# Sums of squares in two fp32r parts, and the first product of merge in the other PSUM bank

## The chip, the cores and the metric

The kernel runs on one core of a Trainium2 chip. What counts is the device time of one launch in microseconds (us). TensorE is called PE in the profile (its weight loads PEld), VectorE is DVE, ScalarE is ACT, GpSimd is POOL, and SyncE is SP, which issues nearly all DMAs.

## The reference

One encoder block in float32, for 1024 tokens and 16 meta tokens with 1024 features. The input is normed and projected; then two branches run side by side, are merged through gates, and a SwiGLU feed-forward block and a last norm follow. Cut to what the change touches:

```
y_a    = (softmax(q1 k1 + bias) - lam * softmax(q2 k2 + bias)) v     # branch A, 4 heads of 128
y_a    = y_a * rsqrt(mean(y_a^2 over the 128 of a head) + EPS) * gain * 0.8
y_b    = windowed attention with sinks, 8 heads of 64                # branch B
merged = sigmoid(ga) * (y_a @ w_ba) + sigmoid(gb) * (y_b @ w_bb)
h      = h + merged @ w_o
```

## The kernel before

**Arithmetic.** TensorE multiplies nearly everything in fp32r, a float32 of reduced precision. To keep the precision of float32, a factor is split into two parts: `split` (L118) has ScalarE copy the high part, rounded to fp32r, and another engine subtract it from the source, which leaves the low part. A product is then three matmuls: high by high, high by low and low by high. The matrix products of the gates, the output and the feed-forward block also go by Strassen-like schemes of seven products, which is where names such as product 1, 6, 5, 7, 3, 4 of a gate come from.

**Branch A** works on four heads `h` and, in each, eight tiles `t` of 128 tokens. For a tile and each of the two softmaxes m, `scores_a` makes 1040 scores in PSUM: two products of 352 columns into the tile `two` (one buffer) and one of 336 into a bank with the tag `sc` (three buffers in turn, which transposes and sums share). VectorE adds the bias and finds the least (L980 for the first 704, L984 for the rest), ScalarE takes the exponential with its sum (L988), VectorE computes the factor (L991, L993) and joins the two softmaxes (L994). `transpose_a` turns the result one tile later, in three banks of `sc` (L1006); ScalarE writes the high part (L1009) and VectorE the low part (L1010) into the tile `at`. `values_a` multiplies by the values, 25 matmuls for two tiles (L1019), and collects 512 tokens, half a head, in the PSUM bank `acc`. `normed_a` then norms that half: it is called eight times.

In `normed_a`, ScalarE squares the bank into `ysq` (L1026) and copies the bank, scaled, into `yg` (L1028). TensorE sums the squares over the partitions by multiplying each 128 columns of `ysq` by a column of ones, in fp32 (L1032). VectorE adds EPS (L1037), POOL takes the power -1/2 (L1038), TensorE spreads the factor over the partitions by four transposes (`apf`, L1043), VectorE multiplies (L1044), and SP stores the half to `ya_d`.

**Gate products** fill the gaps: `gate_steps` yields after three matmuls of 512 columns (L881), and the string `SLOTS` says where between the steps of branch A such a filling stands. POOL makes their weights (L799, L800). Products 5 and 3 of a gate accumulate in one PSUM bank, and 7 and 4 in another; ScalarE copies the bank out after product 5 as `q` (L902), VectorE after 7 (L905) and after 4 (L912).

**Order.** TensorE's order is that of the code (`manual_schedule`). The other engines' order, and that of SP's DMA queue, is made by a scheduler at build time, from its own estimates. Each engine then runs its instructions strictly in that order, and waits at one for what it needs.

**From branch A to merge.** When the last values are done, the pool of branch A is given back, and SP loads the first two weight tiles of branch B's product (L1139) and the eight half rows of y_b (L1142) into the tiles m0 and m1. ScalarE and POOL split the weights (`wbhb`), ScalarE and VectorE split y_b into four tiles `yb0` to `yb3`: `split_yb` does tiles 0 and 1, both halves, before the last gate products, and 2 and 3 behind the closing of the pool `gwork`, from which `ysq` and gate weights come too. Merge then goes through eight feature groups `o` and two token halves: `gated` (L1256) loads a gate, ScalarE takes the Sigmoid (L1260), and TensorE makes 12 matmuls (L721) into a bank that is taken in turn from two sets of four, `bank` and `bank_t`:

```
        n_gated[0] += 1
        ps = (ps_bank if n_gated[0] % 2 else ps_bank_t)(f"ppa_{o}_{half}_{i}")
        branch_mm(ps, w, src, tk)
```

These sets lie where branch A had its banks. After merge the output projection (L1537) begins with four banks of `bank`.

Of the kernel before, what the change touches and what calls it, by code (L numbers as in the profile page):

```python
# [19 lines left out]
P = 128  # L20
S = 1024
D = 1024
NM = 16
# [51 lines left out]
def encoder_block(ctx: ExitStack, tc: tile.TileContext, x, meta, norm_mix, w_in, lq1, lk1, lq2, lk2,  # L75
# [7 lines left out]
    def f32(ap):  # L83
        return ap.bitcast(F32)
# [24 lines left out]

    ident = const.tile([P, P], F32, name="ident")  # L110
    make_identity(nc, ident)
    ones = const.tile([P, 1], F32, name="ones")
    nc.gpsimd.memset(ones, 1.0)
    neg_half = const.tile([P, 4], F32, name="neg_half")
    const.tile([P, ROOM], F32, name="room")
    nc.gpsimd.memset(neg_half, -0.5)
# [881 lines left out]
    def transpose_a(h, t, s, at_):  # L998
        i = t % 2
        for b in range(3):  # L1000
            nb = 4 if b < 2 else 1
            kp = P
            pt = bank(psum2, "sc", f"apt_{h}_{t}_{b}", SC).rearrange("p (k t) -> p k t", k=4)
            for j in range(nb):
                k = 4 * b + j
                nc.tensor.transpose(pt[:kp, j, :], s[:, k * P:k * P + kp], ident)  # L1006
            hi = at_[:kp, 4 * b:4 * b + nb, 0, i * P:(i + 1) * P]
            lo = at_[:, 4 * b:4 * b + nb, 1, i * P:(i + 1) * P] if b < 2 else hi[:NM]
            nc.scalar.activation(hi, pt[:kp, :nb], AF.Copy)  # L1009
            nc.vector.tensor_tensor(lo, pt[:lo.shape[0], :nb], f32(hi)[:lo.shape[0]], ALU.subtract)  # L1010
            yield

    def values_a(h, t, v, at_, py):
        cols = slice(t % 4 // 2 * 256, t % 4 // 2 * 256 + 256)
        for part in range(3):
            for k in range(3 * part, 3 * part + 3):
                kp = P
                for j, (a, b) in enumerate(((0, 0), (0, 1), (1, 0)) if k < 8 else ((0, 0),)):
                    nc.tensor.matmul(py[:, cols], v[:kp, a, k, :], at_[:kp, k, b, :],  # L1019
                                     start=(k == 0 and j == 0), stop=(k == 8))  # L1020
            yield

    def normed_a(h, c, py):
        nm = f"{h}_{c}"
        ysq = gwork.tile([P, 512], F32, tag="ysq", name=f"ysq_{nm}", bufs=1)
        nc.scalar.activation(ysq, py, AF.Square)  # L1026
        yg = gstage.tile([P, 512], F32, tag="yg", name=f"yg_{nm}", bufs=2)
        nc.scalar.activation(yg, py, AF.Copy, scale=gsub)  # L1028
        yield
        pst = bank(psum2, "sc", f"apst_{nm}", SC)  # L1030
        for i in range(4):
            nc.tensor.matmul(pst[:, i:i + 1], ysq[:, i * P:(i + 1) * P], ones, start=True, stop=True)  # L1032
        f = small.tile([P, 4], F32, tag="af", name=f"af_{nm}", bufs=2)
        sums = sum_a.pop((h, c))
        e = small.tile([P, 4], F32, tag="ae", name=f"ae_{nm}", bufs=2)
        nc.vector.scalar_tensor_tensor(e, sums, EPS, sums, ALU.mult, ALU.mult)
        nc.vector.scalar_tensor_tensor(f, pst[:, 0:4], 1.0 / P, e, ALU.mult, ALU.add)  # L1037
        nc.gpsimd.tensor_tensor(f, f, neg_half, ALU.pow)  # L1038
        for _ in range(N_WAIT):
            yield  # L1040
        pf = bank(psum2, "sc", f"apf_{nm}", SC)
        for i in range(4):
            nc.tensor.transpose(pf[:, i * P:(i + 1) * P], f[:, i:i + 1].broadcast_to([P, P]), ident)  # L1043
# [40 lines left out]
    for n in range(AH * NT + T_LAG):  # L1084
        scoring, turning = iter(()), iter(())
        if n == 1:
            fill(2)
        if n < AH * NT:
            h, t = divmod(n, NT)
            if t == 0:  # L1090
                if not h:
                    ensure_g(2)
                ld = load_a(h)
                if not h:
                    ensure_g(4)
                load_v(h, ld[2])
                fill(G_HEAD if h else G_FIRST)
                if not h:
                    turn_into(2)
                    order_pool.__exit__(None, None, None)  # L1100
            if t % 2 == 0:
                at_ = apool.tile([P, 9, 2, 256], F32R, tag="at", name=f"at{h}_{t}", bufs=AT_BUFS)
# [34 lines left out]
    a11, asum, a12, w11 = m0[:, 0], m0[:, 1], m1[:, 0], m1[:, 1]  # L1137
    for o, raw in enumerate((a11[:, 2], asum[:, 0])):
        nc.sync.dma_start(raw.rearrange("p (c n) -> p c n", n=P), w_bb[:, o * P:(o + 1) * P].rearrange("(c p) n -> p c n", p=P))  # L1139
    for j in range(4):  # L1140
        for h in range(2):
            nc.sync.dma_start((a12, w11)[h][:, j], yb_d[j // 2][j % 2 * P:j % 2 * P + P, h * 512:h * 512 + 512])  # L1142
    ypool, close_ypool = pool("ypool")
    first_w = [branch_w(ypool, o, w_bb, "b", raw) for o, raw in enumerate((a11[:, 2], asum[:, 0]))]
# [4 lines left out]
    first_gt = [gate_tile(f"gt_0_{o}") for o in range(2)]  # L1149
    yb_t = []  # L1150

    def split_yb(p, j0):
        for j in (j0, j0 + 1):
            yb_t.append(p.tile([P, 2, S], F32R, name=f"yb{j}"))
        for h in range(2):
            cols = slice(h * 512, h * 512 + 512)
            for k in (j0, j0 + 1):
                split(yb_t[k][:, 0, cols], yb_t[k][:, 1, cols], (a12, w11)[h][:, k], nc.vector)

    ybpool, close_yb = pool("ybpool")  # L1160
    split_yb(ybpool, 0)
    while tail:
        step_tail()
        fill(1)
# [1 line left out]
        fill(1)  # L1166
    close_gwork()
    ybpool2, close_yb2 = pool("ybpool2")
    split_yb(ybpool2, 2)
    order_pe.__exit__(None, None, None)  # L1170
    fill(1000)
    close_psum2()
# [83 lines left out]
    def gated(i, o, half, w, src):  # L1256
        tk = slice(half * 512, half * 512 + 512)
        gt = first_gt.pop(0) if first_gt else gate_tile(f"gt_{i}_{o}_{half}")
        nc.sync.dma_start(gt, g_d[8 * i + o][:, tk])
        gate_ops.append(nc.scalar.activation(gt, gt, AF.Sigmoid))  # L1260
        n_gated[0] += 1
        ps = (ps_bank if n_gated[0] % 2 else ps_bank_t)(f"ppa_{o}_{half}_{i}")
        branch_mm(ps, w, src, tk)
        return gt, ps, tk

# [68 lines left out]
    sums_a.__exit__(None, None, None)  # L1334

    with tc.issue_after(gate_ops[-1].ins):
        nc.scalar.activation(small.tile([P, 1], F32, tag="rstd", name="silu_of_one"), ones, AF.Silu)
    close_ya()
    close_ypool()

# [530 lines left out]
```

## Time and profile before

| what | value |
|---|---|
| median of 3 runs | 1422.95 us (1422.85 to 1427.37) |
| the profiled execution | 1424.24 us |
| its span, first to last instruction | 1421.9 us |
| TensorE busy | 1401.0 us, 99% |
| VectorE, ScalarE, POOL busy | 914.8, 672.1, 636.7 us |
| granted TensorE clock | 0.998 |

The profile is that of one execution, so terms are summed against 1424.24 us. A row of the timeline has the start in us, the duration, the engine, the line, the operation, the written tile and the read ones, the shape and the count; in square brackets stands the idle time of that engine just before, and what ended it. A row with x4 stands for four such instructions one after the other.

### The profile page before, as it was taken

Reading aid. Unit: us, or ns where it says so; the run is one execution under the profiler, and the core shown is the slowest. Engines: PE = TensorE matmul, PEld = TensorE weight load, DVE = VectorE, ACT = ScalarE, POOL = GpSimd, SP = SyncE. Lnnn points to the kernel's source line nnn. Section 1 sums busy time; section 2 is a strip of 40 time slices with the busy share of each in tenths; the row PEclk is TensorE's granted clock in tenths of the full one; section 3 lists DMA queues with packets and bytes.
Section 4 is the critical chain, followed back from the end, with each engine's and each line's share of the span. In section 5 each row is a group of like instructions: output and inputs, shape, how many; then the busy total and the mean of one; then the engine's idle time right before and its main releaser. Section 6 shows DMA issues by size and latency. Waiting matters only on the chain.

```text
span 1421.9 us, 20667 instructions
## 1 busy us (share of the span) xinstructions
PE 1401.0 (99%) x7183; PEld 1202.7 (85%) x7183; DVE 914.8 (64%) x1584; ACT 672.1 (47%) x1284; POOL 636.7 (45%) x648
## 2 busy tenths in 40 slices
PE   9999999998999999999999999999999999999998
PEld 8998999987888888878888888888888888888886
DVE  6555666527787878666978956544555453787566
ACT  6355556435445555455346644333333333444454
POOL 4156865546677666322503055555545441000442
PEclk9999999999999999999999999999999999999999
DMA  8446565386896363296522724433333323954343
GB/s 235 92 128 184 154 199 160 106 290 225 259 318 211 105 209 105 68 342 198 149 103 90 207 90 148 148 106 98 101 111 104 97 97 110 353 186 144 120 128 144
DMA packets 194297, 228.27 MB, mean 161 GB/s; under 512 B 16824, under 2 KB 127360, under 8 KB 194192
## 3 DMA queue, kind: packets, MB, share of 16 engines
q1 hardware_dynamic: 192272, 224.11, 49.3%
q10 hardware_dynamic: 1920, 2.83, 0.7%
q8 instruction: 57, 0.93, 0.3%
q14 instruction: 48, 0.39, 0.1%
HBM read 152.48 MB, written 67.86 MB: 155 GB/s over the span
## 4 chain that ended last, share of the span: by engine, by line
PE 90%; DVE 4%; DMA 2%; ACT 1%; issue 1%; SPq 1%; POOL 1%; ACTq 0%; POOLq 0%; DVEq 0%
PE pg L1634 29%; PE pd L1738 14%; PE pg L881 8%; PE ppa L721 6%; PE po L1537 4%; PE pp_va L230 3%; PE pp_ka L230 3%; PE aps L977 3%; PE pp_qa L230 3%; PE apy L1019 3%; PE pp_qb L230 3%; PE bps L397 2%; PE po L1545 2%; PE bpy L437 1%; PE apt L1006 1%; PE bpt L432 1%
## 5 line engine op out<-in xcount | busy, mean ns | idle before, releaser
L1634 PE MATMUL pg<-t,wop 128*128 128x512 f32 x1056 | 242.5, 389 | 0.0
L1634 PEld LDWEIGHTS pg<-t,wop 128*128 128x128 f32 x1056 | 198.3, 188 | 41.1
L120 POOL TENSOR_TENSOR wop<-wf,wop 128x512 fp32r<-128x512 f32 x114 | 153.9, 1351 | 162.4 <-ACT wop L119 148.7
L1738 PE MATMUL pd<-ob,oa 128*128 128x512 f32 x924 | 210.1, 390 | 0.2 <-DVE ob L120 0.2
L1738 PEld LDWEIGHTS pd<-ob,oa 128*128 128x128 f32 x924 | 173.4, 188 | 36.8 <-DVE ob L120 1.0
L1634 PE MATMUL pg<-b,wop 128*128 128x512 f32 x792 | 183.3, 390 | 0.0
L1634 PEld LDWEIGHTS pg<-b,wop 128*128 128x128 f32 x792 | 148.5, 188 | 30.7
L881 PE MATMUL pg<-hT_hi,wopg 128*128 128x512 f32 x448 | 169.9, 400 | 2.7 <-POOL wopg L800 1.8
L119 ACT ACTIVATE wop<-wf 128x512 fp32r<-128x512 f32 x128 | 80.8, 633 | 73.4 <-PE pg L1634 44.3
L120 POOL TENSOR_TENSOR oa<-ra,oa 128x512 fp32r<-128x512 f32 x27 | 34.9, 1294 | 169.4 <-ACT oa L119 167.7
L119 ACT ACTIVATE oa<-ra 128x512 fp32r<-128x512 f32 x77 | 48.7, 632 | 109.0 <-PE pd L1738 50.8
L988 ACT ACTIVATE as<-as,amn 128x1040 f32<-128x1040 f32 x64 | 74.5, 1165 | 50.6 <-DVE amn L984 50.4
L881 PEld LDWEIGHTS pg<-hT_hi,wopg 128*128 128x128 f32 x448 | 84.3, 188 | 15.5 <-POOL wopg L800 2.2
L1411 DVE TENSOR_TENSOR s<-wf,wf 128x512 f32<-128x512 f32 x22 | 17.6, 798 | 112.2 <-DMA wf<-in_w_ff_up_dram 70.7
L977 PE MATMUL aps<-ak,aq 128*128 128x352 f32 (+1 forms) x384 | 86.6, 334 | 2.4 <-DVE amn L980 2.2
L881 PE MATMUL pg<-hT_lo,wopg 128*128 128x512 f32 x224 | 88.2, 394 | 0.0
L980 DVE CUSTOM_DVE_ANT_0 as<-aps,dist,far_a 128x704 f32<-128x704 f32 x64 | 60.3, 943 | 34.9 <-PE aps L977 34.6
L399 DVE CUSTOM_DVE_ANT_0 bs<-bps,tbx,nsink 128x432 f32<-128x432 f32 (+1 forms) x64 | 38.6, 629 | 61.6 <-PE bps L397 37.8
L1009 ACT ACTIVATE at<-apt 128x512 fp32r<-128x512 f32 (+1 forms) x96 | 45.4, 484 | 63.0 <-PE apt L1006 63.0
L977 PEld LDWEIGHTS aps<-ak,aq 128*128 128x128 f32 x384 | 64.2, 189 | 12.2 <-DVE amn L980 4.7
L409 POOL TENSOR_SCALAR bs<-bs,bdn 128x432 f32<-128x432 f32 (+1 forms) x64 | 36.9, 596 | 75.3 <-DVE bdn L407 34.4
L1019 PEld LDWEIGHTS apy<-at,av 128*128 128x128 f32 x400 | 54.2, 190 | 4.0
(321 smaller groups left out, 3131.1 us busy)
## 6 DMA issues: line engine op xcount, KB each, us to landing
ra<-aop SPq DMA_DIRECT2D x77, 256.0 KB, 2.7
wf<-in_w_ff_gate_dram SPq DMA_DIRECT2D x25, 512.0 KB, 3.8
wf<-in_w_ff_up_dram SPq DMA_DIRECT2D x25, 512.0 KB, 3.8
aop<-as SPq DMA_DIRECT2D x44, 256.0 KB, 2.1
w_c<-in_w_in_dram SPq DMA_DIRECT2D x17, 512.0 KB, 4.8
aop<-c SPq DMA_DIRECT2D x33, 256.0 KB, 2.0
ak<-ka_d SPq DMA_DIRECT2D x16, 520.0 KB, 6.5
t_d<-tst SPq DMA_DIRECT2D x16, 512.0 KB, 3.8
```

Of the source, the lines that this page charges most:

```text
L119: high = nc.scalar.activation(hi, src, AF.Copy)
L120: lo_eng.tensor_tensor(lo, src, f32(hi), ALU.subtract)
L230: product = nc.tensor.matmul(ps[:, :n], a[:, c, :], b[:, c, at:at + n], start=(u == 0), stop=(u == 3 * DC - 1))
L721: nc.tensor.matmul(ps, w[:, a, j, :], src(j, b, tk), start=(j == 0 and n == 0), stop=(j == 3 and n == 2))
L881: nc.tensor.matmul(ps, op[:, x, c, :], h[:, 4 * d + c, HALF[t]], start=(p in (1, 6, 7) and c == 0 and i == 0), stop=(p in (2, 6, 3, 4) and ...
L977: nc.tensor.matmul(ps[:, :n], qs[m][:, t * P:(t + 1) * P], ks[m][:, vv, k0:k0 + n], start=(vv == 0), stop=(vv == 1))
L980: nc.vector.tensor_tensor_reduce(s[m][:, 0:2 * n].rearrange("p (a k) -> p a k", a=2), two[:, :, :n], dist[:, u0:u0 + 2 * n].rearrange("p ( ...
L988: nc.scalar.activation(s[m][:, 0:L], s[m][:, 0:L], AF.Exp, bias=mn[:, m, 1:2], scale=-1.0, accum_out=dn[:, 1:2] if m else first_sum)
L1019: nc.tensor.matmul(py[:, cols], v[:kp, a, k, :], at_[:kp, k, b, :], start=(k == 0 and j == 0), stop=(k == 8))
L1537: nc.tensor.matmul(sets_o[p][u], oa[:, a, u * P:(u + 1) * P], ob[:, b, :], start=(p in (1, 5) and j == 0 and k == 0), stop=(p in (2, 3) an ...
L1634: nc.tensor.matmul(ps, op[:, x, c, :], b[:, y, c, :], start=(p in (1, 5) and c == 0 and n == 0), stop=(p in (4, 2, 3) and c == 3 and n == ...
L1738: nc.tensor.matmul(ps[u], oa[:, a, u * P:(u + 1) * P], ob[:, b, :], start=(p in (1, 2, 5) and j == 0 and k == 0), stop=(p in (2, 3, 4) and ...
```

## The change

- `ones` is a tile of two columns in fp32r.
- In `normed_a` the scaled copy `yg` comes first. Then ScalarE squares the PSUM bank in place, and `split` makes a high and a low part of the squares in `ysq` (twice as large, fp32r): ScalarE copies, VectorE subtracts. TensorE multiplies each 128 columns of both parts by the two columns of ones and accumulates; VectorE reads every second column of the result.
- The tile `at` has 17 slots of 256 columns in place of 18; the slot that is left out was not used.
- The y_b rows are loaded by halves (the first half of all four tiles, then the second), and `split_yb` is called by halves too: tiles 0 and 1, first half, before the last gate products, and behind them tiles 2 and 3 first half, 0 and 1 second half, 2 and 3 second half.
- The banks of merge begin with `bank_t`.

```diff
-    ones = const.tile([P, 1], F32, name="ones")
-    nc.gpsimd.memset(ones, 1.0)
+    ones = const.tile([P, 2], F32R, name="ones")
+    nc.gpsimd.memset(f32(ones), 1.0)
...
-            hi = at_[:kp, 4 * b:4 * b + nb, 0, i * P:(i + 1) * P]
-            lo = at_[:, 4 * b:4 * b + nb, 1, i * P:(i + 1) * P] if b < 2 else hi[:NM]
+            tk = slice(i * P, i * P + P)
+            if b < 2:
+                hi, lo = (at_[:, 8 * b + u:8 * b + 7 + u:2, tk] for u in range(2))
+            else:
+                hi, lo = at_[:, 16:17, tk], at_[:NM, 16:17, tk]
...
-        ysq = gwork.tile([P, 512], F32, tag="ysq", name=f"ysq_{nm}", bufs=1)
-        nc.scalar.activation(ysq, py, AF.Square)
         yg = gstage.tile([P, 512], F32, tag="yg", name=f"yg_{nm}", bufs=2)
         nc.scalar.activation(yg, py, AF.Copy, scale=gsub)
+        nc.scalar.activation(py, py, AF.Square)
+        ysq = gwork.tile([P, 2, 512], F32R, tag="ysq", name=f"ysq_{nm}", bufs=1)
+        split(ysq[:, 0], ysq[:, 1], py, nc.vector)
         yield
         pst = bank(psum2, "sc", f"apst_{nm}", SC)
         for i in range(4):
-            nc.tensor.matmul(pst[:, i:i + 1], ysq[:, i * P:(i + 1) * P], ones, start=True, stop=True)
+            for u in range(2):
+                nc.tensor.matmul(pst[:, 2 * i:2 * i + 2], ysq[:, u, i * P:(i + 1) * P], ones, start=(u == 0), stop=(u == 1))
...
-        nc.vector.scalar_tensor_tensor(f, pst[:, 0:4], 1.0 / P, e, ALU.mult, ALU.add)
+        nc.vector.scalar_tensor_tensor(f, pst[:, 0:8:2], 1.0 / P, e, ALU.mult, ALU.add)
...
-    for j in range(4):
-        for h in range(2):
+    for h in range(2):
+        for j in range(4):
             nc.sync.dma_start((a12, w11)[h][:, j], yb_d[j // 2][j % 2 * P:j % 2 * P + P, h * 512:h * 512 + 512])
...
-    def split_yb(p, j0):
+    def open_yb(p, j0):
         for j in (j0, j0 + 1):
             yb_t.append(p.tile([P, 2, S], F32R, name=f"yb{j}"))
-        for h in range(2):
-            cols = slice(h * 512, h * 512 + 512)
-            for k in (j0, j0 + 1):
-                split(yb_t[k][:, 0, cols], yb_t[k][:, 1, cols], (a12, w11)[h][:, k], nc.vector)
+
+    def split_yb(j0, h):
+        cols = slice(h * 512, h * 512 + 512)
+        for k in (j0, j0 + 1):
+            split(yb_t[k][:, 0, cols], yb_t[k][:, 1, cols], (a12, w11)[h][:, k], nc.vector)
...
-    split_yb(ybpool, 0)
+    open_yb(ybpool, 0)
+    split_yb(0, 0)
...
-    split_yb(ybpool2, 2)
+    open_yb(ybpool2, 2)
+    for j0, h in ((2, 0), (0, 1), (2, 1)):
+        split_yb(j0, h)
...
-        ps = (ps_bank if n_gated[0] % 2 else ps_bank_t)(f"ppa_{o}_{half}_{i}")
+        ps = (ps_bank_t if n_gated[0] % 2 else ps_bank)(f"ppa_{o}_{half}_{i}")
```

More of the change, by code (lines that the diff above doesn't have):

```diff
@@ L1018, in values_a @@
                 for j, (a, b) in enumerate(((0, 0), (0, 1), (1, 0)) if k < 8 else ((0, 0),)):
-                    nc.tensor.matmul(py[:, cols], v[:kp, a, k, :], at_[:kp, k, b, :],
+                    nc.tensor.matmul(py[:, cols], v[:kp, a, k, :], at_[:kp, 2 * k + b, :],
                                      start=(k == 0 and j == 0), stop=(k == 8))
@@ L1101, in encoder_block @@
             if t % 2 == 0:
-                at_ = apool.tile([P, 9, 2, 256], F32R, tag="at", name=f"at{h}_{t}", bufs=AT_BUFS)
+                at_ = apool.tile([P, 17, 256], F32R, tag="at", name=f"at{h}_{t}", bufs=AT_BUFS)
             s = [None, None]
@@ L1336, in encoder_block @@
     with tc.issue_after(gate_ops[-1].ins):
-        nc.scalar.activation(small.tile([P, 1], F32, tag="rstd", name="silu_of_one"), ones, AF.Silu)
+        nc.scalar.activation(small.tile([P, 1], F32, tag="rstd", name="silu_of_one"), f32(ones)[:, 0:1], AF.Silu)
     close_ya()
```

## Prediction

> **What bounds the kernel now.** I read the page first: span, busy time by engine.
>
> ```profile
> span 1421.9 us, 20667 instructions
> PE 1401.0 (99%) x7183; PEld 1202.7 (85%) x7183; DVE 914.8 (64%) x1584; ACT 672.1 (47%) x1284; POOL 636.7 (45%) x648
> ```
>
> TensorE (PE) is the bound nearly everywhere, so an edit counts only by the TensorE work that it removes and by the waits of TensorE that it makes or ends. The second view is the list of TensorE's waits (what waited, for whom, us in total, times, longest).
>
> ```profile
> PE apt L1006 <- DVE at L1010: 2.3, 4, 0.8
> PE aps L977 <- DVE amn L980: 2.2, 7, 0.4
> PE ppa L721 <- DVE g L912: 0.8, 1, 0.8
> ...
> PE pd L1738 <- DVE ob L120: 0.2, 1, 0.2
> ```
>
> The first two lie in branch A, 310 to 597 us: there VectorE (DVE) is at times late, so VectorE has no room in those places. The third is the first product of merge, which the change is aimed at. The third view is the busy time by stretch (stretch, length, PE busy with count, then PEld, DVE, ACT, POOL).
>
> ```profile
> 616.00:700.00 84.00, 84.00 (x372) 69.39 (x371) 62.27 (x82) 38.51 (x68) 29.23 (x19) 1.00 0.69 224
> ```
>
> After 616 us TensorE does not stop (84.00 of 84.00), and of the list's waits only the last, 0.2 us at L1738, lies later. So every microsecond that TensorE loses before 616 us is one at the end: nothing gives it back.
>
> **Part 1: the sums of squares.** There are eight column groups (four heads, two halves), `normed_a` once each. Before: four fp32 products with one column. After: eight fp32r products with two columns. From the timeline, TensorE alone, in one of the middle groups:
>
> ```profile
> 437.32 0.95 PE L1032 MATMUL apst<-ones,ysq 128*128 128x1 f32 x8
> 438.13 0.63 PE L1006 MATMUL apt<-ident,as 128*128 128x128 f32 x4
> ```
>
> The four fp32 products stand there as eight matmuls, and with their weight loads they hold TensorE for 438.13 - 437.32 = 0.81 us, 0.10 each. The trace of before has no fp32r product with so few columns. The nearest rows are these eight themselves (0.10) and the transposes, which also load 128x128 weights per short matmul (four in 0.60 with the drain of the last, as at 441.73 below: at most 0.15 each). So eight after cost about 0.8 too: I take 0. The bounds are a gain of half, 0.4 us a group (3.2 in all), and a loss of 0.1 a group.
>
> [...]
>
> What is added: on ScalarE (ACT) the Copy of the high half, and Square now goes second, behind the scaled copy; on VectorE one subtract of 128x512 from PSUM. All 14 rows that follow are one middle group (head 1, first half) in the timeline:
>
> ```profile
> 432.30 0.60 ACT L1026 ACTIVATE ysq<-apy 128x512 f32<-128x512 f32 x1 [0.93 <-PE apy L1019]
> 432.79 0.69 ACT L1028 ACTIVATE yg<-apy,gsub 128x512 f32<-128x512 f32 x1
> 434.15 0.57 DVE L984 CUSTOM_DVE_ANT_0 as<-aps,far_m,amn 128x336 f32<-128x336 f32 x1
> 434.75 0.69 DVE L905 TENSOR_TENSOR g<-pg,q 128x512 f32<-128x512 f32 x1
> 435.83 0.95 DVE L980 CUSTOM_DVE_ANT_0 as<-aps,dist,far_a 128x704 f32<-128x704 f32 x1 [0.40 <-PE aps L977]
> 436.71 0.69 DVE L1010 TENSOR_TENSOR at<-apt,at 128x512 fp32r<-128x512 f32 x1
> 437.31 0.56 DVE L984 CUSTOM_DVE_ANT_0 as<-aps,far_m,amn 128x336 f32<-128x336 f32 x1
> 437.92 1.16 ACT L988 ACTIVATE as<-as,amn 128x1040 f32<-128x1040 f32 x1 [0.99 <-DVE amn L984]
> 439.20 0.27 DVE L993 TENSOR_SCALAR adn<-asum,adn,neglam 128x1 f32<-128x1 f32 x1 [0.73 <-ACT as L988]
> 439.32 0.88 PE L977 MATMUL aps<-ak,aq 128*128 128x352 f32 x4
> 439.51 1.30 DVE L994 SCALAR_TENSOR_TENSOR as<-as,adn,as 128x1040 f32<-128x1040 f32 x1
> 440.73 0.87 DVE L1010 TENSOR_TENSOR at<-apt,at 128x512 fp32r<-128x512 f32 x2
> 441.73 0.60 PE L1006 MATMUL apt<-ident,as 128*128 128x128 f32 x4
> 442.52 0.91 PE L977 MATMUL aps<-ak,aq 128*128 128x352 f32 x4 [0.19 <-DVE amn L980]
> ```
>
> The squares themselves are in time: scaled copy at 432.30, Square at 432.9, high half by 434.2, low half by 434.9, and `apst` reads them at 437.32, 2.4 us of cover. The price is what stands behind the subtract on VectorE. In the changed program's order it sits just ahead of L984 at 434.15, which moves by 0.7 to 434.85. The 0.40 of idle time before L980 at 435.83 takes up part, and about 0.35 arrives at the exponential (437.92) and at L993 (439.20, now 439.55).
>
> Then comes what the diff doesn't tell. The order of VectorE is made by a scheduler, and with the extra work it turns: in five of the seven middle groups L980 of the next tile now stands ahead of L994 or of the L1010 behind it (before, it stood after both). L980 needs the four score products at 439.32 + 0.88 = 440.20, so it runs 440.2 to 441.2. L994 starts at 441.2 instead of 439.51, L1010 ends at 443.1, and the transposes that wait for its PSUM slot go from 441.73 to 443.1. The score products behind them then needn't wait and start about 0.45 later, at 443.55 instead of 442.52: **+1.0 us**. In the two groups whose order is kept only the 0.35 to 0.5 passes through, I take 0.4. Middle groups: 5 x 1.0 + 2 x 0.4 = +5.8. Bounds: nothing (VectorE's idle time swallows it all), and 7 x 1.5 = 10.5 where a turned L994 also runs long, as this one did beside a POOL instruction:
>
> ```profile
> 366.85 2.25 DVE L994 SCALAR_TENSOR_TENSOR as<-as,adn,as 128x1040 f32<-128x1040 f32 x1
> ```
>
> One small gain: in the last tile L994 no longer stands behind a 16x128 L1010 of 0.27 while TensorE waits, -0.2.
>
> **Part 2: the eighth group and merge's start.** Here nothing but gate products is left to cover waits. The rows run from the last sums to the first product of merge; the last two are the eight loads of yb by source line, with their time from issue to landing.
>
> ```profile
> 600.47 3.88 SPq L1142 DMA_DIRECT2D m<-yb_d  x8
> 601.33 1.01 POOL L1038 TENSOR_TENSOR af<-af,neg_half 128x4 f32<-128x4 f32 x1 [1.22 <-DVE af L1037]
> 602.49 0.63 ACT L119 ACTIVATE wbhb<-m 128x512 fp32r<-128x512 f32 x1 [2.10 <-DMA m<-in_w_branch_b_dram]
> 603.07 0.60 PE L1043 MATMUL apf<-ident,af 128*128 128x128 f32 x4
> 603.20 1.28 POOL L120 TENSOR_TENSOR wbhb<-m,wbhb 128x512 fp32r<-128x512 f32 x1 [0.86 <-ACT wbhb L119]
> 604.68 0.63 ACT L119 ACTIVATE yb<-m 128x512 fp32r<-128x512 f32 x1 [0.74 <-DMA m<-yb_d]
> 607.93 0.56 ACT L902 COPY q<-pg 128x512 f32<-128x512 f32 x1
> 608.89 0.40 PE L881 MATMUL pg<-hT_lo,wopg 128*128 128x512 f32 x1
> 611.40 1.68 ACT L119 ACTIVATE yb<-m 128x512 fp32r<-128x512 f32 x3 [2.31 <-DMA m<-yb_d]
> 613.09 1.28 ACT L1260 ACT_TABLE_LOAD   x1
> 614.38 0.63 ACT L1260 ACTIVATE gt<-gt 128x512 f32<-128x512 f32 x1
> 615.11 25.25 PE L721 MATMUL ppa<-yb,wbhb 128*128 128x512 f32 x110 [0.78 <-DVE g L912]
> L1142 SPq DMA_DIRECT2D m<-yb_d x8: 430/430/499, 600.5 to 603.9; - x8
> DMA to landing us min/median/max: 4.1/5.4/8.1
> ```
>
> Three things move. First, the squares: ready some 1.8 us later, and no cover. Second, on POOL the power (601.33) now stands behind both subtracts for merge's weights, which wait for a load: the first starts at 603.20, so the power ends at 603.2 + 2 x 1.29 + 1.01 = 606.8, and the transposes at 603.07 start at 606.9: +3.8, the first delay inside it. Third, on ScalarE the copy of the gate bank q (607.93) now stands behind the table load, the first Sigmoid and the four copies for yb tiles 2 and 3. TensorE's product (7, 3) accumulates into that bank and waits for the copy. The Sigmoid's input is queued behind the eight yb loads, of which the last lands at 603.9 + 8.1 = 612.0; with one more transfer, 612.6. Sigmoid 0.55, four copies at 1.68 / 3 = 0.56 each, q 0.56: done at about 615.9. The second matmul of (7, 3) goes from 608.89 to 616.1: +7.2, which contains the +3.8.
>
> Merge's first product in the other bank no longer waits for VectorE's L912: -0.78. Its inputs are long split by then. Sum of part 2: +7.2 - 0.8 = **+6.4**. If the Sigmoid's input came much earlier, the power's +3.8 would stay: +3.0 is the lower bound; above, a DMA later by a microsecond gives +7.4.
>
> **At nothing.** The weights tile of 17 slots holds the same slices, so the 400 value products read as before. The last product of merge now lies in the bank of the fourth product of the output projection:
>
> ```profile
> 702.40 12.86 PE L1537 MATMUL po<-ob_o,oa_o 128*128 128x512 f32 x56
> 702.67 0.69 DVE L1299 TENSOR_TENSOR gt<-gt,ppa 128x512 f32<-128x512 f32 x1 [1.52 <-PE ppa L721]
> ```
>
> Nine matmuls (9 x 0.23 = 2.1 us) lie ahead of that fourth product, and VectorE reads the bank by 703.4, 1.0 after 702.40; without the cover it would cost 1.0.
>
> **Sum.** 5.8 - 0.2 + 6.4 = +12.0. The profiled execution took 1424.24 us (2.3 around its span), and would take 1436.2; the median of the three runs lies 1.3 below it, so 1422.95 + 12.0 = 1435.0.
>
> **The rivals.**
> - *Half of it* (one of the two parts is covered): +5.6 or +6.4, so 1428.6 to 1429.4. For it: VectorE is idle for 0.40 and 0.73 in the rows above; against it: TensorE waited for VectorE in these groups before already.
> - *No slower, or a little faster*: the sums' matmuls cost half. That is 8 x 0.4 = 3.2, with merge's wait 4.0: 1419.0. It decides only if the subtract finds idle time in each middle group, and if in the eighth the weight subtracts on POOL start by 599.5 (603.07 - 1.01 - 2 x 1.29) instead of 603.2, with q no later than now. [...] Without the half, the bank alone is 1422.2, which is also the case that the change does nothing else that shows.
> - *Worse*: the turned L994 meets POOL as at 366.85, 0.95 more in each of five groups, +4.8: 1439.8 or above.
>
> **How the numbers follow.** Forecast 0.55, with a range of its own of 1431 to 1439; half 0.20; no slower 0.15; worse 0.10. About 0.3%, 4.3 us, is what a measurement of this kernel can tell from no change: bounds 1418.7 and 1427.2. Faster 0.04 (only the end of the third case), same 0.16 (the rest of it, and the half case where it falls short), slower 0.80. Leaving out the no-slower case and the top of the worst one, the range is 1425 to 1441.
>
> **What would show it.** Right: the wait of `apt` for L1010 in the profile after is several us longer, with L980 run ahead of L994; `apst` still about 0.8 us a group; the power on POOL ends after two weight subtracts; the copy q on ScalarE ends just before the (7, 3) product, with a TensorE wait of some us on it; no wait at merge's first product. Wrong: `apst` at 0.4 us, no longer waits in branch A, or q finished before TensorE asks for it.

## The result, and the profile after

| | us |
|---|---|
| changed kernel, median of 6 runs | 1433.41 (1431.25 to 1434.54) |
| kernel before, median of 6 runs | 1423.29 (1422.52 to 1427.37) |
| ratio | 1.0064, 95% interval 1.0049 to 1.0078 |
| profiled execution after (before) | 1431.29 (1424.24) |

The change costs 0.64%. The forecast of 1435.0 is 1.6 above the median. The profiled execution is one of the two shortest of the six: it shows 7.0 of the 10.1 us by which the medians differ, and the rest has to be found elsewhere (below: the clock).

The page's head, span and TensorE's busy time: TensorE has 1.6 us more of busy time, and waits for the rest.

```profile
span 1429.5 us, 20694 instructions
...
PE 1402.6 (98%) x7183; PEld 1203.8 (84%) x7183; DVE 915.8 (64%) x1592; ACT 675.8 (47%) x1292; POOL 637.7 (45%) x648
```

TensorE's waits after (us in total, times, longest). L1010 is L1013 now.

```profile
PE apt L1006 <- DVE at L1013: 8.0, 8, 1.9
PE apf L1048 <- POOL af L1043: 2.0, 1, 2.0
...
PE ppa L721 <- DVE g L912: 0.8, 1, 0.8
...
PE aps L977 <- DVE amn L980: 0.7, 2, 0.4
PE apt L1006 <- DVE as L994: 0.5, 1, 0.5
```

The wait of `apt` for the subtract of its low part went from 2.3 to 8.0 us, that of `aps` from 2.2 to 0.7, that of `apt` for L994 from 1.7 to 0.5. The wait for the power (`apf`) is new, and so are those for the squares (`apst`) and for q, which stand in the rows further down. Merge's wait for L912 was to go, and is there unchanged.

The timeline after, in the middle group that the prediction worked through (start in us, duration, and in brackets the idle time before):

```profile
437.38 0.95 PE L1037 MATMUL apst<-ones,ysq 128*128 128x2 f32 x8
438.19 0.66 PE L1006 MATMUL apt<-ident,as 128*128 128x128 f32 x4
...
440.34 0.95 DVE L980 CUSTOM_DVE_ANT_0 as<-aps,dist,far_a 128x704 f32<-128x704 f32 x1 [0.70 <-PE aps L977]
...
441.21 1.30 DVE L994 SCALAR_TENSOR_TENSOR as<-as,adn,as 128x1040 f32<-128x1040 f32 x1
442.43 0.87 DVE L1013 TENSOR_TENSOR at<-apt,at 128x512 fp32r<-128x512 f32 x2
...
443.26 0.63 PE L1006 MATMUL apt<-ident,as 128*128 128x128 f32 x4 [1.27 <-DVE at L1013]
443.64 0.89 PE L977 MATMUL aps<-ak,aq 128*128 128x352 f32 x4
```

L980 runs ahead of L994 as foreseen, the transposes start at 443.26 (worked out: 443.1) and the score products behind them at 443.64 (443.55). The sums take 438.19 - 437.38 = 0.81 us, as before.

The timeline after, from the eighth group's sums to merge:

```profile
602.45 0.27 PE L1037 MATMUL apst<-ones,ysq 128*128 128x2 f32 x1 [0.81 <-ACT ysq L119]
603.18 0.94 PE L1037 MATMUL apst<-ones,ysq 128*128 128x2 f32 x7 [0.45 <-DVE ysq L120]
...
605.10 2.52 POOL L120 TENSOR_TENSOR wbhb<-m,wbhb 128x512 fp32r<-128x512 f32 x2 [3.62 <-ACT wbhb L119]
607.58 1.45 POOL L1043 TENSOR_TENSOR af<-af,neg_half 128x4 f32<-128x4 f32 x1
609.09 1.12 PE L1048 MATMUL apf<-ident,af 128*128 128x128 f32 x4 [2.00 <-POOL af L1043]
616.05 0.56 ACT L902 COPY q<-pg 128x512 f32<-128x512 f32 x1
616.66 0.50 PE L881 MATMUL pg<-hT_hi,wopg 128*128 128x512 f32 x1 [0.72 <-ACT q L902]
623.18 1.19 PE L721 MATMUL ppa<-yb,wbhb 128*128 128x512 f32 x4 [0.78 <-DVE g L912]
```

Squares late, power behind two weight subtracts, q just ahead of product (7, 3): all in the order that was forecast. What was not forecast is in the view of stretches (stretch, length, busy times of PE, PEld, DVE, ACT, POOL, then the granted clock, DMA share, GB/s):

```profile
604.00:605.00 1.00, 1.00 (x7) 0.84 (x7) 0.16 (x1) 0.61 (x1) 0.00 (x0) 1.00 0.84 288
605.00:606.00 1.00, 1.00 (x4) 0.80 (x3) 0.00 (x0) 0.56 (x2) 0.90 (x1) 0.61 1.04 240
...
611.00:612.00 1.00, 1.00 (x4) 0.81 (x3) 0.74 (x2) 0.80 (x2) 0.00 (x0) 0.50 1.04 402
612.00:613.00 1.00, 1.00 (x5) 0.79 (x5) 1.00 (x2) 0.98 (x2) 0.00 (x0) 0.98 1.07 404
```

From about 605.2 to 612.0 TensorE's clock is 0.5. That begins some 1.2 us after the sums that waited for the squares; in the kernel before, the clock was 1.0 in the same work.

The start of one and the same matmul in both profiles, subtracted, shows where the time goes. At the first group (346 us) the changed kernel is 0.5 ahead, at the last sums (599) 1.4 behind, at merge 8.1, at the end 7.5. So the seven middle groups cost 1.9 us in this execution, and the eighth with merge's start 6.7, of which 6.1 had come by the last row ahead of the wait for q. For all twelve experiments these differences are in the table below. A clock cut is a stretch at a granted clock of 0.5, as above: 3.4 us in the profiles of sums, halves, last_old, power, qfirst, both, mended, filled and high_pin_bank, 6.8 in those of the changed kernel and of pin.

| kernel | median us | ratio to before | middle groups, us (clock cuts in them) | eighth group and merge's start, us |
|---|---|---|---|---|
| changed | 1433.41 | 1.0064 | +1.9 (0) | +6.7 |
| sums | 1435.38 | 1.0083 | +3.9 (1) | +5.8 |
| halves | 1425.71 | 1.0005 | -0.6 (0) | +1.3 |
| last_old | 1430.50 | 1.0037 | +6.9 (2) | -0.3 |
| high | 1427.86 | 1.0023 | +1.7 (0) | -0.3 |
| power | 1433.77 | 1.0060 | +4.2 (1) | +4.9 |
| qfirst | 1431.51 | 1.0052 | +1.9 (0) | +2.8 |
| both | 1431.86 | 1.0052 | +4.3 (1) | +1.8 |
| bank | 1423.56 | 0.9993 | -0.4 (0) | -0.2 |
| pin | 1429.35 | 1.0042 | +1.8 (0) | +5.2 |
| mended | 1428.34 | 1.0030 | +1.2 (0) | +1.8 |
| filled | 1429.89 | 1.0039 | +3.2 (1) | +1.8 |
| high_pin_bank | 1422.54 | 0.9988 | -0.6 (0) | -1.9 |

Each ratio is to runs of the kernel before on the same chip (medians 1423.29 to 1424.45), and its interval reaches 0.0008 to 0.0017 to either side. The two columns of differences come from one execution each, which need not be a typical one: those of high and qfirst are the shortest of their kernels (1424.45 and 1429.47), that of power is the longest (1434.17). Kernels that change nothing in the middle (halves, bank) show -0.4 to -0.6 there, so that much of a difference means nothing.

### The profile page after: what moved, and what is told of

It reads as the page before. It is cut to its first block, busy times and chain, and to the rows that moved or that the text cites. A ratio compares the mean times of both kernels' runs of the same rounds, so it can differ in the third digit from the quotient of the medians.

```text
span 1429.5 us, 20694 instructions
## 1 busy us (share of the span) xinstructions
PE 1402.6 (98%) x7183; PEld 1203.8 (84%) x7183; DVE 915.8 (64%) x1592; ACT 675.8 (47%) x1292; POOL 637.7 (45%) x648
## 4 chain that ended last, share of the span: by engine, by line
PE 88%; DMA 4%; DVE 4%; issue 1%; ACT 1%; SPq 1%; POOL 0%; ACTq 0%; DVEq 0%; POOLq 0%
PE pg L1643 29%; PE pd L1747 15%; PE pg L881 7%; PE ppa L721 6%; PE po L1546 4%; PE pp_ka L230 3%; PE pp_va L230 3%; PE pp_qa L230 3%; PE aps L977 3%; PE apy L1022 3%; PE apt L1006 2%; PE bps L397 2%; PE pp_qb L230 2%; PE po L1554 2%; PE bpy L437 1%; PE bpt L432 1%
## 5 line engine op out<-in xcount | busy, mean ns | idle before, releaser
L980 DVE CUSTOM_DVE_ANT_0 as<-aps,dist,far_a 128x704 f32<-128x704 f32 x64 | 60.5, 945 | 38.7 <-PE aps L977 38.4
```

The source lines that it names most:

```text
L980: nc.vector.tensor_tensor_reduce(s[m][:, 0:2 * n].rearrange("p (a k) -> p a k", a=2), two[:, :, :n], dist[:, u0:u0 + 2 * n].rearrange("p ( ...
```

## The experiments

**sums: the first part alone.** The kernel before with the new `normed_a`, `ones` and `at`; loads, splits and banks untouched.

> The kernel before with the first part of the change alone: squares in two parts, two columns of ones, the tile at of 17 slots (its room goes to the larger ysq). The loads and splits of yb and the banks are as before. Theory: the whole loss is here, 1431 to 1434 against 1423; POOL's power stands behind both weight subtracts and the copy q behind the table load and four yb copies, though nothing of yb was touched, and the second matmul of product (7, 3) is 7 to 8 us later than before. Rival, the halves of yb make the late q: only the middle groups' loss is left, +1.3 to +3.5, 1424.5 to 1427.

Measured: 1435.38, ratio 1.0083 (1.0066 to 1.0100). The timeline of this kernel:

```profile
611.04 1.47 POOL L1043 TENSOR_TENSOR af<-af,neg_half 128x4 f32<-128x4 f32 x1
...
619.62 0.49 PE L881 MATMUL pg<-hT_hi,wopg 128*128 128x512 f32 x1 [1.64 <-ACT q L902]
```

The power and q are late with nothing of yb touched. So the whole loss lies in the first part of the change, and the scheduler's new orders in the eighth group come from it. The numbers are above the expected ones: the time by 1.4 us, and the product that waits for q comes 11.0 us later than before, of which 5.3 were lost ahead of the eighth group (two clock cuts among them, one between 338 and 344 us and one between 372 and 378).

**halves: the second part alone.**

```diff
-    for j in range(4):
-        for h in range(2):
+    for h in range(2):
+        for j in range(4):
...
+    for j0, h in ((2, 0), (0, 1), (2, 1)):
+        split_yb(j0, h)
```

> The kernel before with the yb rows loaded and split by halves, and nothing else. Theory: the same as before within 1 us (1422.3 to 1424.3); q keeps its place behind the first yb copies on ScalarE and TensorE does not wait for it. Rival, the halves make the late q: +5 to +7, 1428 to 1430.

Measured: 1425.71 against 1424.20, ratio 1.0005 (0.9996 to 1.0014). q keeps its place, but in the profile there is a new wait at product (7, 4):

```profile
612.56 0.68 DVE L905 TENSOR_TENSOR g<-pg,q 128x512 f32<-128x512 f32 x1
613.39 0.47 PE L881 MATMUL pg<-hT_hi,wopg 128*128 128x512 f32 x1 [1.45 <-DVE g L905]
```

L905 stands on VectorE behind a subtract of yb whose load lands late. The halves alone aren't quite free (1.3 in this profile), but by the interval their time can't be told from no change, as expected; nothing like the rival's 5 to 7 us is there. The changed kernel, where q is later, has no such wait in its list.

**last_old: the eighth group in the old form.**

```diff
-            yield from normed_a(h, t // 4, acc[0])
+            yield from (normed_old if (h, t) == (AH - 1, NT - 1) else normed_a)(h, t // 4, acc[0])
```

> The changed kernel with the eighth group alone in the old form (fp32 sums with one column). Theory: the loss of the eighth group and merge's start, 6.7 us, goes, since power and q get their old places; what is left is that of the seven middle groups, 1.3 (all that the two profiles show by 599 us) to 3.5: 1424.5 to 1427. Rival, the middle groups cost what the forecast gave them (+5.6) and the eighth is mostly covered: 1428.5 to 1430.

Measured: 1430.50, ratio 1.0037 (1.0025 to 1.0049). The eighth group's loss is gone (-0.3), as the theory said. Its number failed all the same: the middle groups cost 6.9 us here, and not the 1.9 of the changed kernel's profile. The rival's number (up to 1430) is the nearer one, for another reason. The two profiles have the same wait at the same place, first last_old, then the changed kernel:

```profile
371.97 0.63 PE L1006 MATMUL apt<-ident,as 128*128 128x128 f32 x4 [1.90 <-DVE at L1013]
```

```profile
370.51 0.63 PE L1006 MATMUL apt<-ident,as 128*128 128x128 f32 x4 [1.90 <-DVE at L1013]
```

What follows differs. Stretches of last_old, then of the changed kernel, with the granted clock third from the end:

```profile
372.00:374.00 2.00, 2.00 (x11) 1.86 (x12) 1.22 (x4) 1.36 (x2) 1.97 (x2) 0.83 1.01 409
374.00:376.00 2.00, 2.00 (x7) 1.51 (x7) 2.00 (x7) 0.38 (x2) 0.62 (x2) 0.50 1.03 360
```

```profile
372.00:374.00 2.00, 2.00 (x15) 1.72 (x14) 2.00 (x5) 0.91 (x2) 1.15 (x2) 1.00 1.02 377
374.00:376.00 2.00, 2.00 (x18) 1.87 (x15) 1.72 (x5) 1.61 (x3) 0.45 (x1) 1.00 1.13 349
```

A wait of 1.9 us is followed by a halved clock in one execution and not in another; last_old has a second cut at 414.3. By the table, a cut in the middle costs 2.0 to 2.5 us: 3.9 to 4.3 with one, 6.9 with two, 1.9 with none. The six kernels with the turned order and the subtract had 5 cuts in six profiles, so at 2.2 us each 1.8 on average. An estimate from that: 1.9 + 1.8 + 6.7 = 10.4, less 0.5 that the changed kernel's profile gives back between merge and its end, is 9.9, and the medians differ by 10.1. It is a rough one, since what lies ahead of the first group differs by -0.6 to +2.1 us from profile to profile.

**high: no low part, no work added on VectorE.**

```diff
+        ysq = gwork.tile([P, 512], F32R, tag="ysq", name=f"ysq_{nm}", bufs=1)
         nc.scalar.activation(ysq, py, AF.Square)
...
+            nc.tensor.matmul(pst[:, 2 * i:2 * i + 2], ysq[:, i * P:(i + 1) * P], ones, start=True, stop=True)
```

> The kernel before with the squares rounded to fp32r by Square itself and four products of two columns a group; the low part of the squares is left out, and VectorE and ScalarE have no instruction more than before. In VectorE's order L980 of the next tile stands ahead of L1010 here too. If a product of fp32r takes half of an fp32 one (one matmul for two), a group takes 0.4 instead of 0.81 us, 3.2 less in all. Theory: the order alone makes the new waits for L1010, 0.3 to 0.6 a group, and takes back 1.5 to 4: 1420.5 to 1424. Rival, the subtract makes them: none here, and 1420.0. Rival, small products take the same 0.2 us each in both forms: no gain, 1423 to 1426.

Measured: 1427.86, ratio 1.0023 (1.0013 to 1.0033): slower than before with half the products. A group from the timeline, and the first of the waits:

```profile
436.04 0.50 PE L1032 MATMUL apst<-ones,ysq 128*128 128x2 f32 x4
436.40 0.66 PE L1006 MATMUL apt<-ident,as 128*128 128x128 f32 x4
```

```profile
PE apt L1006 <- DVE at L1010: 11.5, 10, 2.2
```

Four products take 436.40 - 436.04 = 0.36 us in place of 0.81, so one fp32r product (0.09) is the price of one of the two matmuls of an fp32 product (0.10). The gain, 0.45 a group, was there and was more than lost: 11.5 us of waits for L1010 with no instruction added. That VectorE's order makes these waits is shown by the last experiment, which has the same products with the order of before: 3.6 us in place of 11.5, and -0.6 in the middle groups in place of +1.7. The theory had the sign and not the size. This profile is the shortest of twelve executions, 3.4 us below their median, and has no cut among the groups; what the others lost was not seen.

**power: the power ahead of the weight subtracts.**

```diff
+    with tc.issue_after(powers[-1].ins):
+        first_w = [branch_w(ypool, o, w_bb, "b", raw) for o, raw in enumerate((a11[:, 2], asum[:, 0]))]
```

> The changed kernel with POOL's power of the eighth group ahead of the two weight subtracts. Without being told to, the copy q now stands right behind the first Sigmoid, ahead of the four yb copies. Theory, the later wait contains the earlier one: TensorE's 2.0 us wait for the power goes, but the end moves only by what q moves, from 616.6 to about 614.6: -2.0, 1431.4. Rival, the losses add up (the wait 2.0, and what the granted clock of 0.5 behind it costs, about 2.3): -4.3, 1429.

Measured: 1433.77, ratio 1.0060 (1.0046 to 1.0073), from the changed kernel's 1.0064 not to be told apart, and above both expected numbers. In its profile:

```profile
611.17 1.05 PE L1050 MATMUL apf<-ident,af 128*128 128x128 f32 x4
...
618.21 0.57 ACT L902 COPY q<-pg 128x512 f32<-128x512 f32 x1
...
618.83 0.50 PE L881 MATMUL pg<-hT_hi,wopg 128*128 128x512 f32 x1 [1.41 <-ACT q L902]
```

The wait for the power is gone, and the wait for q has grown from 0.7 to 1.4. The eighth group costs 4.9 in place of 6.7, 1.8 less: what q moved (2.0 expected), not the 4.3 of the rival. A clock cut in the middle (+4.2 there) took it back in this execution.

**qfirst: q ahead of the Sigmoids.** The splits of yb stand behind q, and the Sigmoids behind them.

```diff
     fill(1000)
+    with tc.issue_after(q_copies[-1].ins):
+        for j0, h in ((2, 0), (0, 1), (2, 1)):
+            last_high = split_yb(j0, h)
```

> The changed kernel with the copy q ahead of the Sigmoids and of six yb copies on ScalarE; the power stays behind the weight subtracts. TensorE no longer waits for q at product (7, 3). By the prediction 3.8 of 7.2 stay in the tail: -3.4, 1430.0. Rival, the clock: in the profile of the changed kernel TensorE was 7.4 us behind the kernel before already at 612.1, since the granted clock was 0.5 from 605.4 to 612, and the wait for q added 0.7 only: -0.7, 1432.7.

Measured: 1431.51, ratio 1.0052 (1.0038 to 1.0066), between the two expected numbers. In the profile, the eighth group costs 2.8, nearer to the prediction's 3.8 than to the rival's 6. The clock cut was half as long here (606.1 to 609.5), and TensorE, slowed by it, arrived at the transposes when the power was there:

```profile
609.49 0.41 PE L883 MATMUL pg<-hT_hi,wopg 128*128 128x512 f32 x1
609.74 0.60 PE L1050 MATMUL apf<-ident,af 128*128 128x128 f32 x4
```

Neither the wait for the power nor that for q is left, and the loss of the power and that of the clock lie in one another.

**both: power and q first, and another bank for merge.** The edits of power, qfirst and bank together.

> The changed kernel with the power first, q first, and one tile of the other set of banks taken ahead, so that merge's first product really lies in another bank than the last gate product. Theory: of the tail only the squares' delay is left (1.8, as the wait at apst), and merge's wait of 0.78 is gone: 1433.4 - 6.7 + 1.8 - 0.8 = 1427.7. With a clock cut behind the wait at apst alone, as much as 1.7 more: 1429.4. Rival, these orders are not what the time went for: 1431 or above.

Measured: 1431.86, ratio 1.0052 (1.0039 to 1.0065). The eighth group costs +1.8, between the theory without a clock cut behind the sums (1.8 - 0.8 = 1.0) and with all of one (2.7, 1.7 more being half of 3.4 us); there was one. The time itself is the rival's (1431 or above): in this profile the excess lies in the middle groups, 4.3 us with one cut, and not in the eighth.

**bank: really another bank, in the kernel before.**

```diff
+    ps_bank_t("ahead")
```

> The kernel before with one tile of the second set of banks taken ahead, so that merge's first product lies in bank 4 and not in bank 0, where the last gate product lies. (In the change, the two names only changed places: a set gets its addresses at its first request, so the first product stayed in bank 0.) Theory: the wait for L912 at the first product of merge is gone, -0.78: 1422.5. Rival, its inputs are as late: another releaser takes its place in the list of waits, and the time stays 1423.3.

Measured: 1423.56 against 1424.45, ratio 0.9993 (0.9984 to 1.0002). Merge's first product in this profile, with no wait, and a wait that is new:

```profile
609.42 0.50 PE L881 MATMUL pg<-hT_hi,wopg 128*128 128x512 f32 x1 [1.01 <-ACT q L902]
...
614.99 1.31 PE L721 MATMUL ppa<-yb,wbhb 128*128 128x512 f32 x5
```

So another bank does take merge's wait away, but in this profile q came later, behind a copy of yb that waited for its load on ScalarE until 608.26 (607.39 before), and the wait for it took the gain back: -0.2 is left, and the time can't be told from no change. The change itself doesn't take the step. It swaps two names, and the set that is asked first gets the first banks under either name; the wait of 0.8 for L912, there before and after and gone only where the other set is asked ahead, fits that.

**pin: VectorE's order of before, in the changed kernel.** `lows_t` holds the L1010 instructions.

```diff
+                    with tc.issue_after(lows_t[-1].ins) if m and t % 4 == 3 and (h or t > 3) else ExitStack():
                         nc.vector.tensor_tensor_reduce(s[m][:, 0:2 * n]...
```

> The changed kernel with VectorE's order of before: in the seven middle groups L980 of the next tile is queued behind the last L1010 again. (On ScalarE, q now stands ahead of the table load, as in the run with q first, 1431.5, which is the one to compare with.) Theory, the order makes the middle groups' loss: the waits for L1013 fall from 8 us to 2 to 3, TensorE is at most 0.5 us behind the kernel before at the last tile's transposes, and with the stalls the clock cuts of the middle stage go: 1427.5 to 1429.7. Rival, the subtract itself makes it, whatever stands behind it (0.4 a group by the prediction's kept groups, 2.8 in all): 1431 or above, waits of 5 us and more.

Measured: 1429.35, ratio 1.0042 (1.0029 to 1.0055). The time is in the theory's range, and the first two waits in its list are:

```profile
PE apt L1009 <- DVE at L1016: 3.2, 4, 1.1
PE aps L979 <- DVE amn L983: 2.4, 7, 0.4
```

Its interval overlaps that of qfirst (1.0052), the run to compare with. And TensorE loses 1.8 us over the middle groups, which the theory put at 0.5 at most, and as much as with the turned order and no clock cut (1.9). The order decides which wait shows, 8.0 and 0.7 or 3.2 and 2.4, and how long the longest is (1.9 or 1.1), and so perhaps whether a cut follows. That cuts are rarer with the kept order (1 in three profiles, against 5 in six) is too few to be called shown.

Where the 1.8 comes from can be read in the fourth middle group, where VectorE's order was never turned. First before, then the changed kernel, then pin:

```profile
477.21 1.30 DVE L994 SCALAR_TENSOR_TENSOR as<-as,adn,as 128x1040 f32<-128x1040 f32 x1
478.65 0.21 POOL L995 COPY as<-as 128x32 f32<-128x32 f32 x1 [1.47 <-DVE as L994]
478.81 1.28 POOL L800 TENSOR_TENSOR wopg<-wg_s,wopg 128x512 fp32r<-128x512 f32 x1
```

```profile
478.18 1.29 POOL L800 TENSOR_TENSOR wopg<-wg_s,wopg 128x512 fp32r<-128x512 f32 x1
478.34 2.23 DVE L994 SCALAR_TENSOR_TENSOR as<-as,adn,as 128x1040 f32<-128x1040 f32 x1
```

```profile
478.33 2.23 DVE L997 SCALAR_TENSOR_TENSOR as<-as,adn,as 128x1040 f32<-128x1040 f32 x1
```

POOL's order has turned too: the weight subtract L800, which stood behind a copy that waits for L994, now stands ahead of it and runs beside L994, and L994 takes 2.2 us in place of 1.3. All nine kernels with the squares in two parts have this row at 2.23 and lose 1.3 us in this group; the five others have 1.30. The rows beside L994 explain pin's other groups as well. In the kernel before, 12 of the 32 L994 take over 1.6 us, and all 12 have a POOL instruction beside them for more than 0.3 us (of the 20 shorter ones, 8 have). By group, pin's shift moves by +0.5, -0.9, +1.5, +1.3, +0.2, -1.0 and 0.0 us: L994 became long in the third and fourth (2.2) and short in the second and sixth (1.3, where it took 2.4 before). Pin puts back VectorE's order and not POOL's, so it doesn't show what the subtract costs by itself.

**mended: the edits of pin, power, qfirst and bank together.**

> All orders of before put back in the changed kernel: VectorE's in the middle groups, the power ahead of the weight subtracts, q ahead of the Sigmoids, and merge's first product really in another bank. Left are the squares in two parts, with their later readiness in the eighth group (1.7 us of waits at its sums) and the halves of yb. Theory: 1424.3 + 1.7 - 0.8 = 1425.2, and up to 1.7 more with a clock cut behind the wait at the sums: 1425.2 to 1426.9. Rival, the two parts cost something of their own (VectorE's subtract in each group): 1428 or above.

Measured: 1428.34, ratio 1.0030 (1.0019 to 1.0042). The theory's number failed and the rival's holds, but not for the rival's reason alone. In the middle, 1.2 stays in this profile, and the fourth group alone takes 1.3, with POOL's order still turned (L994 at 2.23): not all orders of before are back. In the eighth group 1.8 stays, net of what is saved at merge (0.78 of idle time), for the late squares and the clock cut behind them. The halves of yb are in this kernel too. So the 0.3% that stays is not the price of the subtract alone, and a kernel with POOL's order put back as well was not tried.

**filled: products that nobody reads, in place of the wait.**

```diff
+        if (h, c) == (AH - 1, 1):
+            for _ in range(6):
+                nc.tensor.matmul(pst, hT_hi[:, 0, 0:P], hT_hi[:, 0, 0:512], start=True, stop=True)
```

> The kernel with all orders put back, and six products of 512 columns that nobody reads on TensorE ahead of the eighth group's sums, 6 x 0.23 = 1.4 us, where it would wait 0.8 and 0.5 for the squares. Theory, TensorE's idle time makes the clock cut: the granted clock stays at 1.0 between 600 and 620 us, the gate products behind the sums are 0.23 apart, and the time is 1.0 to 1.7 below that of the kernel without the six: 1424.2 to 1425.5. Rival, the cut comes anyway (the sums with two columns keep TensorE as good as idle, or it is a matter of the stretch): clock 0.5 behind the sums as before, and the same time or 0.1 more.

Measured: 1429.89, ratio 1.0039 (1.0027 to 1.0052). A stretch of mended, then one of filled; the sums end at about 605.4 in the one and 607.5 in the other:

```profile
606.00:608.00 2.00, 2.00 (x7) 1.54 (x6) 0.00 (x0) 0.63 (x1) 2.00 (x3) 0.57 0.83 242
```

```profile
608.00:610.00 2.00, 2.00 (x13) 1.64 (x12) 0.00 (x0) 0.63 (x1) 2.00 (x3) 1.00 0.90 264
```

The cut is gone. All seven profiles with the waits at the eighth group's sums (changed, sums, power, qfirst, both, pin, mended) have a cut behind them, and the seven without them, before and filled (where 0.16 us is left of 1.26) among them, have none there. So the theory of the clock held, and its time failed, 1429.89 where mended took 1428.34: the eighth group costs 1.8 in both profiles, since TensorE came sooner to the next thing that was late, a gate copy that stands on VectorE behind a subtract of yb. (The middle groups of this profile have a cut, those of mended none.)

```profile
613.49 0.50 PE L883 MATMUL pg<-hT_hi,wopg 128*128 128x512 f32 x1 [1.29 <-DVE g L914]
```

**high_pin_bank: a version ahead of both.** The edits of high, pin and bank, in the kernel before.

> A version that may beat both: the kernel before with the high part of the squares alone (the low part is left out; four fp32r products of two columns a group), VectorE's order kept as before, and merge's first product really in another bank. Theory: 8 x 0.4 less for the products and 0.78 less at merge, no new wait: 1424.3 - 4.0 = 1420.3. Rival, the time that the products free is lost again to waits for VectorE in the same groups: 1422.5 to 1424.

Measured: 1422.54, ratio 0.9988 (0.9979 to 0.9997), the one kernel here whose interval lies below 1. It leaves out the low part of the squares, so its sums are those of the high part alone. In the middle groups the rival holds: seven times 0.45 us less of products, and the middle is at -0.6, no better than in kernels that change nothing there. Its first two waits say why; they were 2.3 and 2.2 before:

```profile
PE apt L1009 <- DVE at L1013: 3.6, 5, 1.2
PE aps L979 <- DVE amn L983: 3.0, 8, 0.4
```

What is gained lies at the eighth group and merge's start, 1.9 in this profile, where there is no wait left at all.


## Why the prediction was right, and where not

The sign and the sum held, and so did the mechanism at the eighth group. In the middle groups the mechanism was only part of the story, one step failed, and one term was missing.

- **Sums' matmuls (0 taken).** Right: 0.81 us a group before and after, 437.38 to 438.19. That these sums take half, 0.4 us a group less, as the bound and the case "no slower" have it, no run shows: eight fp32r products take the 0.81 of the four fp32 products, which are recorded as eight matmuls, and four alone take 0.36 (high), 0.09 each, so the gain comes with half the products only. The case "no slower" fails with that.
- **Middle groups (+5.8).** This term was mis-sized, and its pattern was not the forecast one. The group worked out row by row came out as written, +1.1 at its score products, 0.7 by the next sums. Taken over all seven, the profile gives 1.9 without a clock cut: 0.1 ahead of the first, then +0.5, 0.0, +0.7, +1.3, +0.1, -0.3 and -0.5. The five groups with the turned order (first, second, third, sixth and seventh) make 0.4 of it together, in place of 5.0. The step that failed is taking one group for all five: in the second and sixth L994 had run long before (2.4 us, beside POOL) and ran 1.3 after, so they had little or nothing to lose, and in the last tile TensorE had waited 1.7 for L994 anyway, so that 1.2 of a delay of 2.6 went into that wait (0.5 after). That is also why the -0.2 for this tile was too small. The largest loss is in the fourth group, whose order on VectorE was kept (0.4 taken): POOL's order turned there, and L994 ran long, which the prediction had only as a rival and only for turned groups.
- **What makes it.** The prediction gave VectorE's turned order as the cause. High against high_pin_bank shows that this order makes waits with no work added. In the changed kernel it is not the main part: pin, with the old order, loses as much, 1.3 of it in the fourth group. High_pin_bank also shows that products taken away gain nothing in these groups, so the reading "VectorE has no room in those places" held.
- **Squares, power and q (+7.2, containing 3.8).** Right in the order of things and near in size: 6.7 to the first product of merge, with merge's wait still in it. The power ended at 609.0 by its row (606.8 worked out, 608.2 with the middle groups' shift of 1.4; the weights landed later, too), and q was done at 616.6 (615.9 worked out, 617.3 with the shift). What differs is where the time went. The prediction leaves 3.4 us for the wait for q; it was 0.7, since the halved clock had cost TensorE most of the rest by then. That the later wait contains the earlier is shown by power and qfirst: with the first gone the second grows, and either alone leaves less than its full price.
- **Merge's first product (-0.78).** This step failed. It read the diff's exchange of names as an exchange of banks, and so does the title. The product stayed where it was, and its wait of 0.8 with it. The bank run shows that a real exchange does take the wait away.
- **At nothing.** The weights' 17 slots show no wait after. The last product's bank was not put to the test, since the banks were not exchanged. The halves of yb were not named there; alone they make one wait of 1.45, in the changed kernel none.
- **Missing.** The granted clock was counted as 1.0 throughout. Behind TensorE's new waits it was 0.5 for 3.4 to 6.8 us. In the eighth group the wait for q, which sets the end there and would be longer without the cut, covers that cost; in the middle nothing does, at 2.0 to 2.5 us a cut. That the sum of the forecast still came within 1.6 us is in part chance: 5.6 was forecast for the middle, and 1.9 plus some 1.8 of cuts is what the runs hold; and -0.78 was taken at merge that did not come.

What stays open: whether a middle wait is followed by a cut differs between executions with the same wait, and no run here sets it; and what the subtract costs when POOL's order is kept as well was not tried.

## What to carry to other kernels

Where one engine waits for another in every group, neither an instruction more nor a product less has its own price (0.45 us a group less of products gained nothing in the middle groups of high_pin_bank): what counts is the next thing that is late, and that can be read from the rows of one group but must be summed over all of them. A static scheduler's new order can cost more than the work that caused it (11.5 us of waits in high, with no instruction added), so compare the orders of every queue, those of engines that the change doesn't touch too, and look up addresses rather than names. When TensorE gains a wait of a microsecond, look at the granted clock behind it (0.50 for 3.4 us or 6.8 here).

## What the runs showed of the hardware that was not expected

TensorE's granted clock falls to 0.50 after waits as short as 0.81 and 0.45 us around eight two-column products (seven of seven profiles with them, none of seven without), and after a single wait of 1.9 us in some executions and not in others (371.97 in last_old, 370.51 in the changed kernel). It stays there for 3.4 us (606.1 to 609.5 in qfirst) or twice that, 6.8 (605.2 to 612.0 in the changed kernel, which had a wait of 2.00 us in it, until 609.09), with products of 512 columns 0.43 us apart in place of 0.23. A cut near 340 us, which kernels of both kinds have (sums, halves, power, filled and high_pin_bank; halves lost 1.8 us there), may also be why one kernel's runs lie 3 to 8 us apart; that is argued, not shown.

VectorE's L994, 128x1040 in float32, takes from 1.3 us to 2.4; every one of over 1.6 us, 12 in the kernel before and 4 in the changed kernel, has a POOL instruction beside it (478.34 in the changed kernel, with L800 of POOL from 478.18), while not every one with a POOL instruction beside it is long (8 of the 20 shorter ones in the kernel before have one for more than 0.3 us).
